# Three token blocks enter the first projection unnormed, and the gate activations run in two parts around their remaking

## The chip, the core and the metric

The kernel runs on one core of a Trainium2 chip. The core has a matrix engine (TensorE, PE), a vector engine (VectorE, DVE), an activation engine (ScalarE, ACT), a general engine (GpSimd, POOL) and one that only issues transfers here (SyncE, SP). Each runs its own instructions and waits on the others by semaphores. The metric is the device time of one execution in microseconds (us).

## What is computed

One layer of a hybrid decoder, for 1024 prompt tokens and 32 decode tokens (8 sequences of 4), model width 1024, all in float32. Cut to what matters here:

```python
h = rmsnorm(x, norm_w)                      # x * rsqrt(mean(x*x) + eps) * norm_w
proj = einsum('btd,dc->btc', h, w_in)       # one projection, 4104 columns
hq, hf, hi, hgate, fq, fk, fv, ff, fgate = split(proj)
hg_o, S = hgrn_chunked(q(hq), k(hf), log_f(hf), v=hi, s0)   # gated linear recurrence
fox_o = fox attention over fq, fk, fv, log_sigmoid(ff + b)  # forgetting softmax attention
hg = rmsnorm(hg_o, hg_norm_w) * silu(hgate)
fx = fox_o * silu(fgate)
y = rmsnorm(x + concat(hg, fx) @ w_out, final_norm_w)
```

The norm of a token is one factor for its whole row, so a projection of `x * norm_w` can be multiplied by that factor afterwards.

## The kernel before

**Tiling.** The prompt is 8 blocks of 128 tokens (`tb` 0 to 7), the decode rows are a ninth. A block of x lies with the model dimension on the partitions, as 8 slices `k` of 128 x 128 (`xts[tb]`). A float32 product is made as three matmuls of rounded parts: `hi` holds the rounded value, `lo` the rest, and `proj` issues `xhi*hi`, `xhi*lo`, `xlo*hi` for each of the 8 slices, 24 matmuls per block and result bank. A weight slice is split into parts by `split` (a copy, L351 or L353, and a subtraction, L354), a token block by `norm_hi`/`norm_lo` (L269, L273).

**Order.** The order of the instructions on each engine is the order of the code (a manual schedule); pools only add waits. In time:

1. The start. `load_x` and `w1.load` transfer x and the first projection's weights (512 columns, `hi` of the reference, values of the recurrence) in four pairs of slices. Block 0 and block 1 enter it unnormed: `quick_hi`/`quick_lo` (L282, L286) make the parts of `x * norm_w`, `quick_sq`/`quick_r` (L290 and eight matmuls against a column of ones) give `rc`, the factor of each token, and the copy out of the bank multiplies by it (L424, L435). Matmuls of 128x128 ones keep PE busy before (`warm`).
2. Blocks 2 to 7 and the decode rows enter normed. `norm_a` squares a block (ACT, L243), multiplies it by norm_w (POOL, L245) and sums the squares per token (DVE, L249); `norm_b` sums over the partitions with one matmul of ones, makes the factor (ACT, L218 and L219), multiplies (DVE, L265) and makes the parts (L269, L273). It stands for the next block after the first nine matmuls of a block.
3. The gate loop, `gate_group(tb)` for blocks 2 to 7, 0, 1: 48 matmuls of 260 columns into two banks, copied out by DVE (L526 the first bank, L529 adds a bias to 8 columns of the second, L530 copies the rest of it). The same two banks serve the next group. Then `again` remakes blocks 0 and 1 with the norm in, in three steps, one behind each of the first six groups: square, norm_w and sums (L304, L306, L307); the sum over the partitions, the factor and the product (L218, L219, L313); the parts (L269, L273). Then `silu_mul` (ACT L379, L380, L381; DVE L382; ACT L383; POOL L384, L386) acts on the gate in place. The first of the 24 slabs of 128 columns is split behind groups 4 and 6 (L486 on ACT, L487 on DVE). After the last group come `log_sigmoid` of the forget gates (L536 to L545) and the gates of the decode rows (`proj_d`, 32 matmuls; L369, L370).
4. The slabs (`slab`, 24 matmuls on each of three stretches of 352 columns), with the recurrence and the attention woven in, then the output. They read the parts of all blocks, normed.

`U(i)` are reused buffers of one kind. `wk` holds `ones` and small sums, and the same buffer is `silu_mul`'s scratch later (in order listings it is `u_103`).

Of the kernel before, what the change touches and what calls it, by code (L numbers as in the profile page):

```python
# [70 lines left out]
def tile_hymba(ctx, tc, x_prompt, x_sample, x_b, x_d, cache_k_t, cache_v, cache_logf_t, state_hgrn, page_table,  # L71
               norm_w, w_1, w_2, w_s, b_fox_f, hg_lb, hg_norm_w, w_out, final_norm_w, consts,
# [54 lines left out]
    def ps_s():  # L127
        return bank("ps", 3)
# [103 lines left out]
    warm(14)  # L232
# [46 lines left out]
    rc = cst.tile([128, 2], F32, name="rc")  # L279
# [52 lines left out]
    class Group:  # L332
# [12 lines left out]
        def split(self, kp, ce=(A, A), se=(V, G)):  # L345
# [3 lines left out]
            for a in range(2):  # L349
# [25 lines left out]
    def silu_mul(x, n):  # L375
# [10 lines left out]
        G.tensor_mul(x3, x3, hw[:n, None, :].to_broadcast([n, NH, HK]))  # L386

# [51 lines left out]
    for tb in range(2, NB):  # L439
        if tb < 6:  # L440
            norm_a(tb + 2)
# [3 lines left out]
        w1.proj(ps, tb, every, range(3))  # L445
# [107 lines left out]
    anew = [again(0), again(1)]  # L553
    for n, tb in enumerate((2, 3, 4, 5, 6, 7, 0, 1)):
        gate_group(tb)
        if n < 6:
            next(anew[n // 3])
# [7 lines left out]
        silu_mul(sg[tb // 2][:, tb % 2], 128)  # L565
# [9 lines left out]
    silu_mul(sgd[:, :512], ND)  # L575
# [981 lines left out]
```

## Time and profile before

| | us |
|---|---|
| runs, three | 773.49, 775.08, 773.97 |
| median | 773.97 |
| profiled execution | 775.96 |
| its span, first to last instruction | 774.20 |
| mean granted clock of PE | 0.985 |

The span is what the profile's times count from; the profiled execution took 1.76 us more. Its rows below are of two kinds. A row of the timeline gives start, length, engine, source line, operation, what is written and read, shape and count, and in brackets how long the engine sat idle before it and who ended that. A row of the waits or of a stretch gives sums.

### The profile page before, as it was taken

The page shows a single profiled execution, that of the slowest core. Times are in us where ns is not written, and L with a number is a line of the kernel's source. Part 1 is how long each engine was busy: PE and PEld are TensorE (multiplying, and loading weights), DVE is VectorE, ACT ScalarE, POOL GpSimd, SP SyncE. Part 2 cuts the span into 40 slices and gives each one's busy share as a digit, 9 for nine tenths or more (in the row PEclk, how much of TensorE's full clock was granted, in tenths as well). Part 3 has the DMA queues.
Part 4 walks back from the last instruction along what each step waited for, and adds up shares of the span by engine and source line. Part 5 has one row for each costly group of instructions (what it writes and reads, how often), then busy time and mean ns, then how long its engine had stood idle before and what let it go on. Part 6 is the DMA issues. An engine that isn't in the chain of part 4 may idle for free.

```text
span 774.2 us, 13013 instructions
## 1 busy us (share of the span) xinstructions
PE 741.8 (96%) x4835; PEld 665.5 (86%) x4835; DVE 464.8 (60%) x973; ACT 363.5 (47%) x853; POOL 315.1 (41%) x332
## 2 busy tenths in 40 slices
PE   8999989999999999998999899989999899999996
PEld 7778989998999999998998899979988776577886
DVE  5775554747647565366447844785478776667422
ACT  5663555434242431136546654757466521555322
POOL 0442544364371753726434552536344533232101
PEclk9999999999999999999999999999999999999999
DMA  8211000101221113013001021101111596713521
GB/s 337 93 36 40 1 11 20 60 4 58 82 83 58 55 33 110 28 37 134 28 29 57 29 71 40 57 30 55 55 57 57 188 329 221 260 58 123 199 81 55
DMA packets 27569, 64.99 MB, mean 84 GB/s; under 512 B 5394, under 2 KB 6546, under 8 KB 27506
## 3 DMA queue, kind: packets, MB, share of 16 engines
q1 hardware_dynamic: 27506, 64.16, 24.3%
q8 instruction: 38, 0.62, 0.3%
q14 instruction: 25, 0.20, 0.1%
HBM read 47.27 MB, written 16.88 MB: 83 GB/s over the span
## 4 chain that ended last, share of the span: by engine, by line
PE 73%; DVE 13%; ACT 8%; issue 3%; DMA 2%; POOL 1%; SPq 1%; DVEq 0%; ACTq 0%; POOLq 0%
PE pj L95 53%; PE ps L95 11%; PE po L95 3%; PE pt L965 2%; DVE u L970 2%; DVE u L896 1%; PE pt L95 1%; DVE st L935 1%; ACT u L969 1%; ACT u L945 1%; DMA u<-in_x_prompt_dram 1%; DMA u<-in_w_dram 1%; ACT xhi L269 1%; DVE u L831 1%; DVE u L638 1%
## 5 line engine op out<-in xcount | busy, mean ns | idle before, releaser
L95 PE MATMUL pj<-xhi,u 128*128 128x352 f32 x1152 | 307.2, 331 | 0.9 <-DVE u L487 0.5
L95 PEld LDWEIGHTS pj<-xhi,u 128*128 128x128 f32 x1152 | 206.5, 190 | 3.1 <-DVE u L487 0.8
L95 PE MATMUL pj<-xlo,u 128*128 128x352 f32 x576 | 187.3, 325 | 0.0
L95 PE MATMUL ps<-u,u 128*128 128x64 f32 (+6 forms) x984 | 129.2, 272 | 3.5 <-ACT u L945 2.6
L95 PEld LDWEIGHTS ps<-u,u 128*128 128x128 f32 (+2 forms) x984 | 112.2, 178 | 12.9 <-ACT u L945 4.4
L950 POOL TENSOR_SCALAR u<-u,st 128x128 f32<-128x128 f32 (+3 forms) x64 | 48.7, 762 | 153.4 <-DVE st L948 87.7
L95 PEld LDWEIGHTS pj<-xlo,u 128*128 128x128 f32 x576 | 109.6, 190 | 0.7
L95 PE MATMUL pj<-u,xhi 128*128 128x260 f32 (+1 forms) x384 | 91.7, 332 | 5.7 <-DVE u L526 3.4
L945 ACT ACTIVATE u<-ps,st 128x512 f32<-128x512 f32 (+2 forms) x96 | 55.0, 578 | 50.3 <-DVE st L938 21.4
L95 PEld LDWEIGHTS pj<-u,xhi 128*128 128x128 f32 x384 | 65.2, 195 | 13.9 <-DVE u L526 3.0
L95 PE MATMUL pj<-h,u 128*128 128x512 f32 (+2 forms) x237 | 74.1, 384 | 0.8 <-DVE h L1086 0.8
L699 POOL TENSOR_TENSOR u<-u,u 128x256 f32<-128x256 f32 (+1 forms) x56 | 42.0, 751 | 76.5 <-PE ps L95 76.4
L970 DVE TENSOR_TENSOR u<-pt,u 128x512 fp32r<-128x512 f32 (+1 forms) x80 | 48.5, 632 | 28.4 <-ACT u L969 27.9
L95 PE MATMUL pj<-u,xlo 128*128 128x260 f32 (+1 forms) x192 | 63.8, 333 | 0.0
L969 ACT ACTIVATE u<-pt 128x512 fp32r<-128x512 f32 (+1 forms) x80 | 41.8, 552 | 41.1 <-PE pt L965 33.5
L935 DVE TENSOR_REDUCE st<-ps 128x1 f32<-128x512 f32 (+2 forms) x96 | 53.4, 556 | 12.2 <-PE ps L95 9.6
L95 PE MATMUL po<-u,u 128*128 128x256 f32 (+1 forms) x320 | 52.2, 287 | 8.5 <-DVE u L970 4.5
L95 PEld LDWEIGHTS po<-u,u 128*128 128x128 f32 x320 | 44.3, 189 | 15.4 <-DVE u L970 7.5
L95 PEld LDWEIGHTS pj<-h,u 128*128 128x128 f32 (+1 forms) x237 | 42.4, 186 | 10.3 <-issue 1.5
L95 PE MATMUL pj<-u,u 128*128 128x512 f32 (+3 forms) x174 | 46.1, 434 | 2.4 <-ACT u L1253 1.0
L95 PE MATMUL pj<-w,u 128*128 128x512 f32 (+2 forms) x125 | 47.4, 380 | 0.0
L700 POOL TENSOR_TENSOR u<-u,u 128x256 f32<-128x256 f32 (+1 forms) x56 | 43.6, 778 | 0.0
(252 smaller groups left out, 1147.0 us busy)
## 6 DMA issues: line engine op xcount, KB each, us to landing
u<-in_w_s_dram SPq DMA_DIRECT2D x24, 512.0 KB
out_dram<-u SPq DMA_DIRECT2D x12, 512.0 KB
u<-in_x_b_dram SPq DMA_DIRECT2D x8, 512.0 KB
u<-in_cache_k_t_dram SPq DMA_DIRECT2D x16, 256.0 KB
u<-in_cache_v_dram SPq DMA_DIRECT2D x16, 256.0 KB
m_s<-u SPq DMA_DIRECT2D x7, 512.0 KB
u<-m_s SPq DMA_DIRECT2D x14, 256.0 KB
w<-in_w_out_dram SPq DMA_DIRECT2D x12, 256.0 KB
```

The source lines that it names most:

```text
L95: PE.matmul(out, lhsT, rhs, start=start, stop=stop, skip_group_check=True)
L269: A.activation(xhi[:, k, t0:t0 + n], xt[:, k], AF.Copy)
L638: V.tensor_mul(f, f3[:, :, 0], f3[:, :, 1])
L699: G.tensor_mul(k4[:, :, 0, :], k4[:, :, 0, :], f3[:, eb, 1:2].to_broadcast([128, n, m]))
L700: G.tensor_mul(q4[:, :, 1, :], q4[:, :, 1, :], f3[:, eb, 0:1].to_broadcast([128, n, m]))
L831: V.tensor_copy(hi, vo[:, :, 64 * i:64 * i + 64])
L935: V.tensor_reduce(st[:, m:m + 1], ps, axis=AX.X, op=OP.min)
L945: A.activation(P[:, s], ps, AF.Exp, scale=-1.0, bias=st[:, lo:lo + 1], accum_out=st[:, 2 + m:3 + m])
L950: G.tensor_scalar(P[:, :e], P[:, :e], st[:, 4:5], 1.0, op0=OP.mult, op1=OP.mult)
L965: PE.transpose(p[:, c:c + 128], probs[n, b][:, j * 128:(j + 1) * 128], ident)
L969: A.activation(ph[:, :w], p[:, :w], AF.Copy)
L970: V.tensor_sub(pl[:, :w], p[:, :w], f32(ph[:, :w]))
```

## The change

Three blocks, 0 to 2, enter unnormed. Blocks 0 and 1 go side by side: for each slice `k` the three matmuls of block 0 are followed by the three of block 1, into two banks, and the weights are split slice by slice, all copies on ACT. Block 1's transfer moves ahead of the second weight pair, and norm_w comes as 8 more columns of block 0's transfer (`x_0`); `nwc` is a copy of it. Neither `quick_sq` nor `quick_r` is left: the results stay unscaled in `v`. The loop over the other blocks starts with block 2, unnormed. `again` now also makes `rc`, by a second matmul into the same bank, and scales `v`; it is there for blocks 0, 1 and 2, one step behind each of groups 1 to 7, with two steps behind groups 3 and 5 (the last of one block and the first of the next). The gate loop takes blocks 3 to 7, 0, 1, 2; block 2's input is transferred a second time. `silu_mul` is a generator: Abs, Exp and Ln are issued before the step of `again`, the rest after it.

```diff
     xts = {}
 
     def load_x(tb):
         n = 128 if tb < NB else ND
-        xts[tb] = U((17, 18, 24, 25, 26, 27, 24, 25, 26)[tb], D, a=KB)[:, :, :n]
-        SP.dma_start(xts[tb], (x_b[tb] if tb < NB else x_d).rearrange("p (k t) -> p k t", k=KB))
+        t = U((17, 18, 24, 25, 26, 27, 25, 26, 27)[tb], D + KB if tb == 0 else D)
+        xts[tb] = t[:, :D].rearrange("p (a b) -> p a b", a=KB)[:, :, :n]
+        if tb == 0:
+            SP.dma_start(t, x_0)
+        else:
+            SP.dma_start(xts[tb], (x_b[tb] if tb < NB else x_d).rearrange("p (k t) -> p k t", k=KB))
+
+
+    nwT = U(17, D + KB)[:, D:]
...
-    rc = cst.tile([128, 2], F32, name="rc")
+    rc = cst.tile([128, 3], F32, name="rc")
...
-    def quick_sq(tb):
-        A.activation(U(15 + tb % 2, D, a=KB), xts[tb], AF.Square)
-
-    def quick_r(tb):
-        sq, p = U(15 + tb % 2, D, a=KB), ps_s()[:, :1]
-        for k in range(KB):
-            mm(p, sq[:, k], ones[:, :1], k == 0, k == KB - 1)
-        rstd(rc[:, tb:tb + 1], p, D)
+    nwc = cst.tile([128, KB], F32, name="nwc")
 
     def again(tb):
 
         xt, sq = xts[tb], U(7, D, a=KB)
-        on, s, r = (U(6)[:, i * 128:i * 128 + 128] for i in range(3))
+        on, s, r = (U(6)[:, i * 128:i * 128 + 128] for i in (0, 2 * tb + 1, 2 * tb + 2))
         if tb == 0:
             V.memset(on, 1.0)
         A.activation(sq, xt, AF.Square)
...
         yield
-        p = ps_s()[:, :128]
-        mm(p, on, s, True, True)
-        rstd(r, p, D)
+        p = ps_s()[:, :129]
+        mm(p[:, :128], on, s, True, True)
+        mm(p[:, 128:], s, on[:, :1], True, True)
+        rstd(r, p[:, :128], D)
+        rstd(rc[:, tb:tb + 1], p[:, 128:], D)
         for k in halves:
             V.tensor_mul(xt[:, k], xt[:, k], r[:, None, :].to_broadcast([128, 4, 128]))
         yield
         for f in (norm_hi, norm_lo):
             for k in halves:
                 f(tb, k)
+        x = v[tb // 2][:, tb % 2]
+        A.activation(x, x, AF.Copy, scale=rc[:, tb:tb + 1])
         yield
...
         A.activation(t, t, AF.Ln, bias=1.0)
+        yield
         V.scalar_tensor_tensor(t, x, 0.0, t, op0=OP.min, op1=OP.subtract)
         A.activation(t, t, AF.Exp)
         G.tensor_mul(x, x, t)
         x3 = x.rearrange("p (h v) -> p h v", h=NH)
         G.tensor_mul(x3, x3, hw[:n, None, :].to_broadcast([n, NH, HK]))
+        yield
...
     load_x(0)
-    SP.dma_start(nwT, norm_w)
     w1.load(0)
+    load_x(1)
     w1.load(1)
-    load_x(1)
     w1.load(2)
     w1.load(3)
-    load_x(2)
-    load_x(3)
-    ks = range(KB)
-    for k in ks:
-        quick_hi(0, k)
-    for k in ks[:4]:
-        quick_lo(0, k)
-    w1.split(0, (V, V), (V, V))
-    quick_sq(0)
-    for k in ks[4:]:
-        quick_lo(0, k)
-    w1.split(1, (A, A), (V, V))
-    load_x(4)
-    load_x(5)
+    for tb in range(2, 6):
+        load_x(tb)
     SP.dma_start(cc, consts[:, :K_MK])
     pa, pb = ps_pj(), ps_pj()
-    w1.proj(pa, 0, every, ks[:4])
-    w1.split(2, (A, A), (V, V))
-    w1.proj(pa, 0, every, ks[4:6])
-    w1.split(3, (A, A), (V, V))
-    quick_r(0)
-    for k in ks:
-        quick_hi(1, k)
-    w1.proj(pa, 0, every, ks[6:])
-    for k in ks:
-        quick_lo(1, k)
-    A.activation(v[0][:, 0], pa, AF.Copy, scale=rc[:, 0:1])
+
+    def quick(tb, *ks):
+        for k in ks:
+            quick_hi(tb, k)
+            quick_lo(tb, k)
+
+    for k in range(0, KB, 4):
+        quick(0, *range(k, k + 4))
+        for i in range(k, k + 4):
+            w1.split(i // 2, (A, A), (V, V), (i % 2,))
+            if i < k + 2:
+                quick(1, i)
+            if i == k + 1:
+                quick(1, k + 2, k + 3)
+            w1.proj(pa, 0, every, (i,))
+            w1.proj(pb, 1, every, (i,))
+    V.tensor_copy(nwc, nwT)
+    quick(2, *range(KB))
+    norm_a(3)
+    A.activation(v[0][:, 0], pa, AF.Copy)
     w2.load(0)
     w2.load(1)
-    red = norm_sq(2)
-    quick_sq(1)
-    red(0)
-    w1.proj(pb, 1, every, ks)
-    norm_b(2)
-    quick_r(1)
-    norm_a(3)
-    load_x(6)
-    A.activation(v[0][:, 1], pb, AF.Copy, scale=rc[:, 1:2])
+    A.activation(v[0][:, 1], pb, AF.Copy)
     w2.load(2)
     SP.dma_start(bf, bcast_row(b_fox_f, FH))
     SP.dma_start(hw, bcast_row(hg_norm_w, HK))
     for tb in range(2, NB):
-        if tb < 6:
+        if 2 < tb < 6:
             norm_a(tb + 2)
         if tb == 7:
             w1.proj_d(vd, every)
         ps = ps_pj()
-        w1.proj(ps, tb, every, range(3))
+        w1.proj(ps, tb, every, range(4 if tb == 2 else 3))
         if tb == 6:
             norm_b(NB)
         if tb < 7:
             norm_b(tb + 1)
-        if tb < 4:
-            load_x(tb + 5)
+        if tb == 2:
+            norm_a(4)
+        if tb < 5:
+            load_x(tb + 4)
         if tb == 5:
             norm_a(NB)
-        w1.proj(ps, tb, every, range(3, 6))
+        w1.proj(ps, tb, every, range(4 if tb == 2 else 3, 6))
         if tb < 5:
             w2.split(tb - 2)
         if tb == 3:
...
-    anew = [again(0), again(1)]
-    for n, tb in enumerate((2, 3, 4, 5, 6, 7, 0, 1)):
+    anew = [again(tb) for tb in range(3)]
+
+    xts[2] = U(2, D, a=KB)
+    SP.dma_start(xts[2], x_b[2].rearrange("p (k t) -> p k t", k=KB))
+    for n, tb in enumerate((3, 4, 5, 6, 7, 0, 1, 2)):
         gate_group(tb)
-        if n < 6:
-            next(anew[n // 3])
+        si = silu_mul(sg[tb // 2][:, tb % 2], 128)
+        next(si)
+        for i in range(3):
+            if 2 * i <= n <= 2 * i + 2:
+                next(anew[i])
         if n == NB - 1:
             log_sigmoid(lf.rearrange("p b h -> p (b h)"), zf.rearrange("p b h -> p (b h)"), 128, 64)
             V.tensor_copy(lfh, lf.rearrange("p b h -> p h b"))
@@ -562,7 +562,7 @@
             w2.proj_d(sgd[:, 260:], slice(260, 520))
         if n in (3, 4, 5):
             next(lbs)
-        silu_mul(sg[tb // 2][:, tb % 2], 128)
+        next(si)
```

Two places on ACT, one on PE and one on DVE show what moved.

ACT at the start of the program, before (`u_121` and `u_128` are blocks 0 and 1, `u_126`, `u_130`, `u_132` weight pairs 2 to 4, whose first pair DVE splits):
```order
L282 ACTIVATE xhi<-u_121,nwT 128x128 x8
L290 ACTIVATE u_154<-u_121 128x1024
L351 ACTIVATE u_160<-u_126 128x512 x2
L351 ACTIVATE u_183<-u_130 128x512 x2
L351 ACTIVATE u_195<-u_132 128x512 x2
L218 ACTIVATE rc<-ps_202,eps 128x1
```

and after (`u_72` is block 0 with norm_w, `u_124` block 1, `u_122`, `u_126`, `u_128` pairs 1 to 3):
```order
L287 ACTIVATE xhi<-u_72 128x128 x4
L353 ACTIVATE u_147<-u_122 128x512
L287 ACTIVATE xhi<-u_124,u_72 128x128
L353 ACTIVATE u_147<-u_122 128x512
L287 ACTIVATE xhi<-u_124,u_72 128x128 x3
L353 ACTIVATE u_173<-u_126 128x512 x2
L287 ACTIVATE xhi<-u_72 128x128 x4
L353 ACTIVATE u_199<-u_128 128x512
```

Block 1's parts stand between the copies of the weights, and the square and the factor are gone.

PE, the end of block 0 in the start, before (`pj` are result banks, `u_103` holds the column of ones, `u_154` the squares):
```order
L95 MATMUL pj_170<-u_183,xlo 128x512
L95 MATMUL ps_202<-u_103,u_154 128x1 x8
L95 MATMUL pj_170<-u_195,xhi 128x512
L95 MATMUL pj_170<-u_196,xhi 128x512
L95 MATMUL pj_170<-u_195,xlo 128x512
```

and its first six matmuls after `warm` in the changed kernel:
```order
L95 MATMUL pj_138<-u_147,xhi 128x512
L95 MATMUL pj_138<-u_148,xhi 128x512
L95 MATMUL pj_138<-u_147,xlo 128x512
L95 MATMUL pj_137<-u_147,xhi 128x512
L95 MATMUL pj_137<-u_148,xhi 128x512
L95 MATMUL pj_137<-u_147,xlo 128x512
```

The eight one-column matmuls are gone, and two banks take turns slice by slice.

DVE, the fourth group of the gate loop up to the emptying of the fifth's first bank, before (`u_627` and `u_628` squares and sums, `u_831` the slab's high part):
```order
L526 COPY u_101<-pj_169 128x260
L529 TENSOR_TENSOR zf<-pj_170,bf 128x8
L530 COPY u_101<-pj_170 128x252
L307 TENSOR_REDUCE u_628<-u_627 128x128
L511 TENSOR_TENSOR lb<-lb 128x4
L382 SCALAR_TENSOR_TENSOR u_103<-u_101,u_103 128x512
L487 TENSOR_TENSOR u_832<-u_124,u_831 128x512
L526 COPY u_102<-pj_169 128x260
```

and after:
```order
L520 COPY u_102<-pj_137 128x260
L523 TENSOR_TENSOR zf<-pj_138,bf 128x8
L524 COPY u_102<-pj_138 128x252
L313 TENSOR_TENSOR u_124<-u_124,u_613 128x512 x2
L505 TENSOR_TENSOR lb<-lb 128x4
L385 SCALAR_TENSOR_TENSOR u_103<-u_102,u_103 128x512
L481 TENSOR_TENSOR u_826<-u_122,u_825 128x512
L520 COPY u_102<-pj_137 128x260
```

The products of block 1's second step stand there instead of its first step's sums.

ACT, the seventh group of the gate loop and the start of the eighth's activations, before (`u_99` is their gate buffer):
```order
L379 ACTIVATE u_103<-u_99 128x512
L380 ACTIVATE u_103<-u_103 128x512
L381 ACTIVATE u_103<-u_103 128x512
L383 ACTIVATE u_103<-u_103 128x512
L536 ACTIVATE u_128<-zf 128x64
```

and after (`u_556` is block 2, `u_96` its projection):
```order
L381 ACTIVATE u_103<-u_99 128x512
L382 ACTIVATE u_103<-u_103 128x512
L383 ACTIVATE u_103<-u_103 128x512
L274 ACTIVATE xhi<-u_556 128x4x128 x2
L319 ACTIVATE u_96<-u_96,rc 128x512
L386 ACTIVATE u_103<-u_103 128x512
L381 ACTIVATE u_103<-u_100 128x512
```

The high parts of block 2 are written here, behind the seventh group's Ln; the eighth group is block 2's. In the eighth group Abs, Exp and Ln now stand ahead of the log-sigmoid.

## Rows read from the trace of the kernel before

**Rows 1.** The page: busy us of each engine, its share, instructions.
```profile
PE 741.8 (96%) x4835; PEld 665.5 (86%) x4835; DVE 464.8 (60%) x973; ACT 363.5 (47%) x853; POOL 315.1 (41%) x332
```

**Rows 2.** Gate loop and decode rows: busy PE, PEld, DVE, ACT, POOL; clock; DMA.
```profile
68.70:124.40 55.70, 52.29 (x421) 51.91 (x420) 30.73 (x62) 25.80 (x47) 24.63 (x19) 0.97 0.03 11
```

**Rows 3.** PE's waits up to 130 us: total, times, longest.
```profile
PE pj L95 <- DVE u L526: 3.4, 2, 2.8
```

**Rows 4.** Three stretches, columns as in rows 2; the clock is third from the end.
```profile
10.20:13.60 3.40, 3.27 (x8) 2.07 (x8) 3.38 (x9) 1.91 (x4) 0.00 (x0) 0.50 1.02 416
27.20:30.60 3.40, 3.40 (x9) 2.26 (x8) 2.76 (x3) 2.70 (x5) 2.11 (x3) 0.50 0.51 143
102.30:105.70 3.40, 3.40 (x19) 3.40 (x18) 2.03 (x7) 2.56 (x6) 0.94 (x1) 0.50 0.00 0
```

**Rows 5.** Timeline of the start: start us, us, engine, line, operation.
```profile
4.76 2.45 ACT L282 ACTIVATE xhi<-u,nwT 128x128 fp32r<-128x128 f32 x8 [2.74 <-DMA nwT<-in_norm_w_dram]
...
7.72 0.43 DVE L353 CAST u<-u 128x512 fp32r<-128x512 f32 x1 [1.30 <-DMA u<-in_w_dram]
...
9.00 1.15 ACT L351 ACTIVATE u<-u 128x512 fp32r<-128x512 f32 x2 [0.85 <-DMA u<-in_w_dram]
...
10.90 3.89 DVE L354 TENSOR_TENSOR u<-u,u 128x512 fp32r<-128x512 f32 x6
...
17.88 2.40 DVE L286 SCALAR_TENSOR_TENSOR xlo<-u,nwT,xhi 128x128 fp32r<-128x128 f32 x8 [3.08 <-ACT xhi L282]
...
18.36 0.62 PE L95 MATMUL pj<-u,xhi 128*128 128x512 f32 x2
...
19.05 0.63 PE L95 MATMUL pj<-u,xhi 128*128 128x512 f32 x2
...
24.12 1.84 PE L95 MATMUL ps<-u,u 128*128 128x1 f32 x16
...
40.21 0.30 PEld L95 LDWEIGHTS pj<-u,xhi 128*128 128x128 f32 x2 [0.35 <-ACT xhi L269]
```

**Rows 6.** Timeline of the gate loop and the decode rows, several engines.
```profile
74.69 0.17 DVE L529 TENSOR_TENSOR zf<-pj,bf 128x8 f32<-128x8 f32 x1 [2.00 <-issue]
...
75.28 0.64 ACT L379 ACTIVATE u<-u 128x512 f32<-128x512 f32 x1 [4.85 <-DVE u L530]
...
77.27 0.69 DVE L382 SCALAR_TENSOR_TENSOR u<-u,u 128x512 f32<-128x512 f32 x1
...
80.61 0.37 ACT L218 ACTIVATE u<-ps,eps 128x128 f32<-128x128 f32 x1 [1.98 <-PE ps L95]
...
81.42 1.30 DVE L313 TENSOR_TENSOR u<-u,u 128x512 f32<-128x512 f32 x2 [0.54 <-POOL u L386]
...
84.47 1.14 ACT L269 ACTIVATE xhi<-u 128x512 fp32r<-128x512 f32 x2
...
90.21 1.04 ACT L304 ACTIVATE u<-u 128x1024 f32<-128x1024 f32 x1
...
92.53 2.03 DVE L307 TENSOR_REDUCE u<-u 128x128 f32<-128x1024 f32 x1
...
99.11 1.34 DVE L487 TENSOR_TENSOR u<-u,u 128x512 fp32r<-128x512 f32 x1 [1.21 <-ACT u L486]
...
99.98 1.61 POOL L386 TENSOR_TENSOR u<-u,hw 128x512 f32<-128x512 f32 x1
...
100.84 0.51 PE L95 MATMUL pj<-u,xhi 128*128 128x260 f32 x2 [2.79 <-DVE u L526]
...
120.61 4.00 PE L95 MATMUL pj<-u,xd 128*64 128x260 f32 x32
...
120.81 0.17 DVE L529 TENSOR_TENSOR zf<-pj,bf 128x8 f32<-128x8 f32 x1 [2.46 <-PE pj L95]
...
121.59 0.20 DVE L538 TENSOR_SCALAR u<-u 128x64 f32<-128x64 f32 x1 [0.29 <-ACT u L537]
...
123.89 0.41 DVE L370 TENSOR_TENSOR sgd<-sgd,pj 32x260 f32<-32x260 f32 x1
```

More of the change, by code (lines that the diff above doesn't have):

```diff
@@ L70, in tile_hymba @@
 @with_exitstack
-def tile_hymba(ctx, tc, x_prompt, x_sample, x_b, x_d, cache_k_t, cache_v, cache_logf_t, state_hgrn, page_table,
-               norm_w, w_1, w_2, w_s, b_fox_f, hg_lb, hg_norm_w, w_out, final_norm_w, consts,
+def tile_hymba(ctx, tc, x_prompt, x_sample, x_0, x_b, x_d, cache_k_t, cache_v, cache_logf_t, state_hgrn, page_table,
+               w_1, w_2, w_s, b_fox_f, hg_lb, hg_norm_w, w_out, final_norm_w, consts,
                y_prompt, y_sample, k_t, prompt_v, prompt_logf, prompt_state,
@@ L180, in need @@
         debt[0] = max(debt[0], -3.0)
-    A.preload_act_table_set("natural_log_exp_and_others")
-    nwT = cst.tile([128, KB], F32, name="nwT")
     xts = {}
@@ L188, in load_x @@
         n = 128 if tb < NB else ND
-        xts[tb] = U((17, 18, 24, 25, 26, 27, 24, 25, 26)[tb], D, a=KB)[:, :, :n]
-        SP.dma_start(xts[tb], (x_b[tb] if tb < NB else x_d).rearrange("p (k t) -> p k t", k=KB))
+        t = U((17, 18, 24, 25, 26, 27, 25, 26, 27)[tb], D + KB if tb == 0 else D)
[5 more added lines that the diff above has]
+    nwT = U(17, D + KB)[:, D:]
+    A.preload_act_table_set("natural_log_exp_and_others")
     cc = cst.tile([128, K_MK], F32, name="cc")
@@ L230, in warm @@
             mm(pw[:, :128], ones, ones, True, True)
-    warm(14)
+    warm(13)
     ss_ = {}
@@ L244, in norm_sq @@
         for k in (slice(0, 4), slice(4, 8)):
-            G.tensor_mul(xt[:, k], xt[:, k], nwT[:, k, None].to_broadcast([128, 4, n]))
+            G.tensor_mul(xt[:, k], xt[:, k], nwc[:, k, None].to_broadcast([128, 4, n]))
         def reduce(a):
@@ L305, in again @@
         for k in halves:
-            G.tensor_mul(xt[:, k], xt[:, k], nwT[:, k, None].to_broadcast([128, 4, 128]))
+            G.tensor_mul(xt[:, k], xt[:, k], nwc[:, k, None].to_broadcast([128, 4, 128]))
         V.tensor_reduce(s, sq.rearrange("p k t -> p t k"), axis=AX.X, op=OP.add)
         yield
-        p = ps_s()[:, :128]
-        mm(p, on, s, True, True)
-        rstd(r, p, D)
+        p = ps_s()[:, :129]
[3 more added lines that the diff above has]
+        rstd(rc[:, tb:tb + 1], p[:, 128:], D)
         for k in halves:
@@ L343, in load, with split @@
             SP.dma_start(raw, self.w[kp].rearrange("p (a c) -> p a c", a=2))
-        def split(self, kp, ce=(A, A), se=(V, G)):
+        def split(self, kp, ce=(A, A), se=(V, G), parts=(0, 1)):
             raw = self.raw[kp]
@@ L348, in split @@
             l = U(self.hl[2 * kp + 1], 2 * self.n, F32R, a=2)
-            for a in range(2):
+            for a in parts:
                 if ce[a] is A:
@@ L574, in tile_hymba @@
         G.tensor_copy(m8[:, l], mk[:, l:l + 1].to_broadcast([128, 4, 64]))
-    silu_mul(sgd[:, :512], ND)
+    for _ in silu_mul(sgd[:, :512], ND):
+        pass
     def log_forget():
@@ L1523, in pairs @@
         return a.reshape(4, 2, 128, -1).transpose(0, 2, 1, 3).reshape(4, 128, -1)
+    x_b = np.asarray(x_prompt)[0].reshape(NB, 128, KB, 128).transpose(0, 3, 2, 1).reshape(NB, 128, D)
     ins = dict(
         x_prompt=x_prompt, x_sample=x_sample,
-        x_b=np.asarray(x_prompt)[0].reshape(NB, 128, KB, 128).transpose(0, 3, 2, 1).reshape(NB, 128, D),
+        x_0=np.concatenate([x_b[0], np.asarray(norm_w).reshape(KB, 128).T], 1), x_b=x_b,
         x_d=np.asarray(x_sample).reshape(ND, KB, 128).transpose(2, 1, 0).reshape(128, KB * ND),
@@ L1532 @@
         state_hgrn=np.asarray(state_hgrn)[0].transpose(1, 2, 0, 3).reshape(NH, 128, DB * 128),
-        page_table=page_table, norm_w=np.asarray(norm_w).reshape(KB, 128).T,
+        page_table=page_table,
         w_1=pairs(w[:, C_HI:C_HI + 512]),
```

## The prediction, made before the changed kernel ran

> **What bounds the kernel now.** I read the page first: TensorE (PE) is busy 741.8 us, 96% of the span [rows 1], so a microsecond is won or lost only where PE idles or runs at half its clock. The change touches the first 125 us. In the gate loop and the decode rows behind it PE is busy 52.29 of 55.70 us [rows 2]. The list of PE's waits up to 130 us names that loop's own: 3.4 us in two waits, 2.8 the longest, for VectorE (DVE) line 526, the copy that empties a gate bank [rows 3]. [...] The timelines of the start [rows 5] and of the gate loop [rows 6] give the durations.
>
> **The start.** Removed: two sums of squares, 16 records of one-column matmuls each, 1.84 us a time [rows 5], 3.7 us on PE's path. Moved: block 1's input lands in the slot where the second weight pair landed. The chain to the first matmuls is then: first pair there at 7.7; ScalarE (ACT) copies slice 0 (two took 1.15, say 0.6 each) to 8.3; block 1 there at 9.0, its first high part to 9.4; slice 1's copy to 9.95; its low part on DVE, 0.65 (six took 3.89), to 10.65. By then PE has done 7 of the 48 matmuls of blocks 0 and 1; before it DVE has 11 low parts of x at 0.30 and 6 of weights at 0.65, done at 17.9, and ACT 11 at 0.31 and 6 at 0.6, done at 17.0 [rows 5]. PE takes longer: three matmuls start in 0.69 (18.36 to 19.05), 0.23 each, and twice that at half clock. I keep the half-clock stretch 10.2 to 13.6, since PE idles before it as now [rows 4]: 6 matmuls to 13.6, the other 35 in 8.05, end 21.65. PE, not the splitting, sets this end; it needs the last slice at 20.3. Copying out block 0 ends 0.2 later and holds block 2, which is unnormed too and has its parts ready by then. Block 2 takes 24 x 0.23 and 0.15 for a sum, to 27.5. Block 3's norm starts behind 12 of its matmuls and needs about 2.6: there at 27.2, no wait. Then a wait: block 4's square follows block 3's high parts on ACT (27.8 + 1.04 [rows 6]), its reduce takes 2.03 on DVE, so its sum is there at 30.9, and PE reaches it behind nine matmuls of block 3 at 29.6: 1.3 idle. Fifteen matmuls more and the 0.35 wait that block 4 has now: it starts at 34.85, against 40.21 [rows 5], **5.4 us earlier**. Cross-check: 3.7 of one-column matmuls and 1.7 of the half-clock stretch 27.2 to 30.6 behind the second of them make 5.4. Blocks 4 to 7 keep order and pace. Bounds: 3.6 if the clock falls behind the new 1.3 wait (1.7 less), 8.4 if that wait and the first half-clock stretch both go (1.3 and 1.7 more). norm_w now rides in block 0's rows, and ACT's first copy waited 2.74 for its landing [rows 5], but what PE needs next is the weight pair at 7.7: nothing. The copy of norm_w, one warming matmul fewer and the reload of block 2 (on the queue of SyncE ahead of the first slab, which is split only in the fourth group) lie beside longer work: nothing.
>
> **The gate loop.** The change reorders the queues of DVE and ACT, and each of these engines waits at the head of its queue. Call E the moment DVE adds the bias (line 529) of a group, which first reads the second bank. PE's own pace is 48 matmuls, 5.7 us a group; E goes from 74.69 to 120.81 over seven groups, 46.1 us with the waits and one half-clock stretch [rows 6]. Now ACT's Abs, Exp and Ln stand ahead of every step of the remaking. They begin 0.6 behind E (74.69 to 75.28), and Ln ends at E + 2.6 (DVE's product starts at 77.27). Before, the remaking had that time. Behind E + 2.6 the steps add up so [rows 6]:
> - sum step (groups 2, 4, 6): Ln and Exp for r 0.7, two multiplications 1.30, the gate's product 0.6: E + 5.3, then the next bank is emptied. In group 2 this is inside PE's own time (6.1 with the sums). In groups 4 and 6 the first slab's split stands behind: final Exp 0.63, copy 0.6, subtraction 1.34, emptying 0.37; the next E is at +8.4 and +8.3.
> - write-and-square step (groups 3 and 5): high parts 1.14, the new scaling of v 0.55 (half of that pair, the nearest row), square 1.04, reduce 2.03, product 0.6, emptying 0.37: +8.2, and +8.9 with four small lower-bound operations.
> - group 1: square, reduce and product behind Ln: +6.6.
> - group 7: the block remade in it (block 2) is the very one that group 8 reads. PE is done at E - 0.3, needs the first half of the high part, E + 3.2, then waits 0.5 more for the low part; 5.74 of matmuls and 0.27 to DVE: +9.7.
>
> Sum: 6.6 + 6.1 + 8.2 + 8.4 + 8.9 + 8.3 + 9.7 = 56.2 against 46.1, **10.1 us more**. The same sums for the order of before give 44.3, with its half-clock stretch 46.0, so I give them 1.5 either way. In groups 3 to 6 DVE's queue is the bound: the emptying copy is queued behind multiplications and a reduce that wait for ACT, and PE waits for the copy. **The tail**: the log-sigmoid's ACT part comes behind Ln (DVE takes it up at E + 3.2) instead of at E + 0.8 (121.59 - 120.81), so the bank that slab 0 needs is emptied at E + 5.9 instead of E + 3.5 (123.89 + 0.41 - 120.81), while PE's 32 decode matmuls end near 124.4, E + 3.6: **2.3 us more**. In slab 0 ACT has less left to do: 0 to 0.5 back, I take 0.3. **The clock**: now PE's 2.79 idle [rows 6] is followed by a half-clock stretch [rows 4], already in the 46.1. The changed loop has waits of 2 to 3 in groups 3 to 6, where a slow PE hides behind DVE, 5.6 before group 8 and 2.3 before slab 0; behind these two PE is the bound. Between 0 and 3.4; I take 3.2, nearest to what followed the 2.79.
>
> Sum: -5.4 + 10.1 + 2.3 - 0.3 + 3.2 = **+9.9 us**. The profiled execution took 775.96, 1.76 around its span of 774.20; the median of the runs shown, 773.97, is 2.0 below it, and I add the difference to the median: 783.9. The ends of all terms together are +2 (start 8.4, loop 8.6, no clock loss) and +14 (start 3.6, loop 11.6).
>
> **Rivals.** (a) Faster: DVE empties the banks in time. If the multiplications' wait for ACT does not hold groups 3 to 6, their waits go, those of now too (2.8 and 0.6, and 1.7 of clock), and group 8's wait of 4.0 and the tail stay: -5.4 - 5.1 + 4.0 + 2.3 + 0.5 of clock = -3.7, 770.3. It decides at whether the next bank is emptied by E + 5.7. For it: ACT is busy only 25.80 of 55.70 [rows 2], and a slip in the order of events would count in four groups. Against it: the subtraction of 99.11 alone made DVE so late that PE stood 2.79 us until 100.84 [rows 6], and it stays. 0.07. (b) Half hidden: groups 3 to 6 cost 4.5 to 9.5 us less, because the sums stack waits that overlap: 774.4 to 779.4. 0.15. (c) The start doesn't do what it says: PE waits slice by slice for ACT and DVE, and the clock stays low for a second stretch; 3.5 of the gain go: 787.4. For it: ACT's weight copies queue behind its wait for block 1. Against it: 17.9 against 20.3 above. 0.10. (d) GpSimd beside DVE: a 128x512 subtraction took 1.34 (99.11) with a GpSimd product next to it (99.98), where six took 0.65 each [rows 5, 6]. If six more of DVE's two-input operations in the loop fall so, 0.65 each, the chain grows by 3.9: 787.8. Against it: GpSimd's two products follow the final Exp, when DVE mostly copies or reduces. 0.08. The forecast has the other 0.60.
>
> [...]
>
> **How the numbers follow.** A measurement of this kernel can tell about 0.2%, 1.5 us, from no change. Faster by more: (a), 0.07. Within it, 772.4 to 775.5: the low end of (b), 0.04. Slower: 0.89. The range reaches from inside (b) to just beyond (c) and (d), 776.5 to 788.5; it leaves out (a), the low part of (b) and the far ends of (c) and (d).
>
> **What would show it.** Block 4's first matmul near 35 us and no one-column records before it, or the start's step is wrong. E of the first and of the eighth group 56 us apart; PE's waits in the loop led by the high part of the remade block, 5 to 6 us at once, and by the emptying copy; slab 0's first matmul 2 to 3 us late for the decode rows' addition. If the eight E lie 46 to 50 apart, the queue argument is wrong, and so is the sign.

## The result, and the profile of the changed kernel

The changed kernel takes 781.64 us (median of 4 runs, 779.46 to 782.50) against 773.73 for the kernel before: a ratio of 1.0096, 95% interval 1.0071 to 1.0121, 7.9 us slower. The forecast was 9.9 us slower. The profiled execution of the changed kernel is the lowest of its four (779.46, its span 777.7), while that of before (775.96) lay 2.2 above the median of 773.73; the two profiles therefore differ by only 3.5 us, and the terms below are compared place by place.

First the page and the stretches, columns as in [rows 1], [rows 2] and [rows 4]: the gate loop with the decode rows, the stretch that ran at half clock before, and the two that do so now.

```profile
PE 738.9 (95%) x4807; PEld 662.2 (85%) x4807; DVE 465.5 (60%) x980; ACT 366.9 (47%) x866; POOL 314.6 (40%) x332
```

```profile
61.19:130.40 69.21, 59.08 (x429) 57.39 (x427) 32.98 (x68) 33.41 (x65) 26.05 (x21) 0.90 0.05 19
10.20:13.60 3.40, 3.40 (x17) 2.64 (x16) 3.40 (x10) 3.40 (x11) 0.00 (x0) 1.00 1.04 418
...
115.60:119.00 3.40, 3.34 (x14) 3.11 (x15) 1.90 (x3) 1.77 (x4) 0.72 (x1) 0.50 0.02 5
119.00:122.40 3.40, 3.40 (x19) 3.40 (x19) 0.43 (x1) 0.00 (x0) 1.84 (x2) 0.57 0.00 0
```

PE has lost 2.9 us of busy time and the kernel is slower. In the loop it idles 10.1 of 69.2 us, against 3.4 of 55.7 in [rows 2]. The stretch from 10.2 to 13.6 holds 17 matmuls at full clock where [rows 4] had 8 at half. PE's waits up to 135 us, as in [rows 3], name new causes beside the emptying copy (line 520 now): the high parts of a remade block, 3.3 us at once, the reduce of the remaking, and the decode rows' addition.

```profile
PE pj L95 <- ACT xhi L274: 3.6, 2, 3.3
PE pj L95 <- DVE u L520: 2.6, 4, 1.1
PE ps L95 <- DVE u L305: 2.4, 2, 1.4
PE pj L95 <- DVE sgd L372: 2.0, 1, 2.0
```

The timeline of the start, to be read beside [rows 5]:

```profile
5.76 0.63 ACT L353 ACTIVATE u<-u 128x512 fp32r<-128x512 f32 x1
...
6.45 0.50 PE L95 MATMUL pj<-u,xhi 128*128 128x512 f32 x1
...
27.92 0.49 PE L95 MATMUL ps<-u 128*128 128x128 f32 x2 [0.97 <-DVE u L254]
...
31.95 0.73 PE L95 MATMUL pj<-u,xhi 128*128 128x512 f32 x2
...
33.34 0.50 PE L95 MATMUL pj<-u,xlo 128*128 128x512 f32 x1 [0.66 <-DVE xlo L278]
```

The copy of the first weight slice begins at 5.76, so that pair had landed by then; before, its copy waited until 7.72. Block 4 starts at 31.95 against 40.21. Now DVE's timeline of the gate loop, its additions of the bias only (the moment E of each group):

```profile
67.22 0.17 DVE L523 TENSOR_TENSOR zf<-pj,bf 128x8 f32<-128x8 f32 x1 [2.52 <-PE pj L95]
...
73.64 0.15 DVE L523 TENSOR_TENSOR zf<-pj,bf 128x8 f32<-128x8 f32 x1
...
79.85 0.17 DVE L523 TENSOR_TENSOR zf<-pj,bf 128x8 f32<-128x8 f32 x1 [0.80 <-PE pj L95]
...
87.92 0.15 DVE L523 TENSOR_TENSOR zf<-pj,bf 128x8 f32<-128x8 f32 x1
...
95.96 0.15 DVE L523 TENSOR_TENSOR zf<-pj,bf 128x8 f32<-128x8 f32 x1
...
104.61 0.16 DVE L523 TENSOR_TENSOR zf<-pj,bf 128x8 f32<-128x8 f32 x1
...
112.57 0.15 DVE L523 TENSOR_TENSOR zf<-pj,bf 128x8 f32<-128x8 f32 x1
...
124.70 0.17 DVE L523 TENSOR_TENSOR zf<-pj,bf 128x8 f32<-128x8 f32 x1 [2.71 <-PE pj L95]
```

From the third to the seventh the steps are 8.07, 8.04, 8.65 and 7.96 where PE alone needs some 6, and only three of the eight additions stand behind a wait for PE: DVE reaches the others without one, straight from the work before them in its queue. The last step is 12.13. The chain of waits shows its links (start, us, what):

```profile
115.09 0.53 ACT xhi L274
...
115.66 9.01 PE pj L95 x48
...
127.25 0.15 ACT u L530
...
130.09 0.33 DVE sgd L372
130.41 0.04 issue
130.46 0.59 PE pj L95 x2
```

The kernel before at two of these places, the first matmul of its eighth group and of slab 0:

```profile
114.78 0.48 PE L95 MATMUL pj<-u,xhi 128*128 128x260 f32 x2 [0.63 <-DVE u L526]
...
124.44 0.34 PE L95 MATMUL pj<-xhi,u 128*128 128x352 f32 x1
```

ACT begins block 2's high parts at 115.0, behind the seventh group's Ln; PE starts the eighth group at 115.66, and its addition follows 9.0 us later (124.70), where it took 6.0 before (114.78 to 120.81): the low clock costs 3.0. Slab 0 starts at 130.46, 5.76 behind the last addition, against 3.63 before (124.44 - 120.81).

Where the time went, from the two profiles: the start gives 7.47 at the first addition (74.69 to 67.22), the loop takes 11.36 more (57.48 against 46.12), the tail 2.13 more; slab 0 starts 6.02 later. Behind it the code is the same, and these two executions differ by 2.5 the other way (649.8 and 647.2 us): 0.9 are two waits of PE near slab 0 that are gone, the rest is not the change's doing as far as the runs show.

### The profile page after: what moved, and what is told of

Same layout as the page of the kernel before. It is cut to its first block, busy times and chain, and to the rows that moved or that the text cites. A ratio compares the mean times of both kernels' runs of the same rounds, so it can differ in the third digit from the quotient of the medians.

```text
span 777.7 us, 12973 instructions
## 1 busy us (share of the span) xinstructions
PE 738.9 (95%) x4807; PEld 662.2 (85%) x4807; DVE 465.5 (60%) x980; ACT 366.9 (47%) x866; POOL 314.6 (40%) x332
## 4 chain that ended last, share of the span: by engine, by line
PE 65%; DVE 14%; ACT 5%; issue 2%; POOL 1%; DVEq 0%; ACTq 0%; POOLq 0%
PE pj L95 46%; PE ps L95 11%; PE po L95 3%; PE pt L966 2%; DVE u L897 2%; DVE u L971 2%; DVE st L936 2%; PE pt L95 1%; ACT u L946 1%; ACT u L970 1%; DVE u L853 1%; DVE u L832 1%; DVE u L998 1%; DVE u L639 1%; DVE ps L935 0%
## 5 line engine op out<-in xcount | busy, mean ns | idle before, releaser
L95 PE MATMUL pj<-xhi,u 128*128 128x352 f32 x1152 | 304.1, 328 | 2.0 <-DVE sgd L372 2.0
L95 PEld LDWEIGHTS pj<-xhi,u 128*128 128x128 f32 x1152 | 204.3, 188 | 3.9 <-DVE sgd L372 2.2
L95 PE MATMUL ps<-u,u 128*128 128x64 f32 (+7 forms) x952 | 125.7, 273 | 3.5 <-ACT u L946 2.6
L95 PEld LDWEIGHTS ps<-u,u 128*128 128x128 f32 (+2 forms) x952 | 108.4, 178 | 12.9 <-ACT u L946 4.4
L95 PE MATMUL pj<-u,xhi 128*128 128x260 f32 (+1 forms) x384 | 93.7, 337 | 6.6 <-ACT xhi L274 3.6
L95 PEld LDWEIGHTS pj<-u,xhi 128*128 128x128 f32 x384 | 67.4, 202 | 14.7 <-ACT xhi L274 5.3
L95 PEld LDWEIGHTS po<-u,u 128*128 128x128 f32 x320 | 44.3, 188 | 16.2 <-DVE u L971 7.6
```

Of the source, the lines that this page charges most:

```text
L95: PE.matmul(out, lhsT, rhs, start=start, stop=stop, skip_group_check=True)
```

## The experiments

**e1: the gate activation whole again, behind the remaking step.** Start, third block and spread stay.

```diff
         si = silu_mul(sg[tb // 2][:, tb % 2], 128)
-        next(si)
         for i in range(3):
...
             next(lbs)
+        next(si)
         next(si)
```

> The gate activation is whole again and stands behind the remaking step, as before the change; the new start, the third remade block and the spread over seven groups stay. Theory (order of ACT's queue): the loop lost its 11.4 us because Abs, Exp and Ln stand ahead of each remaking step. Then the eight additions of the bias lie 46.6 us apart by the same sums, 48.3 with one half-clock stretch, instead of 57.5; the log-sigmoid is ahead of the gate activation again, so slab 0 starts 3.6 us behind the last of them instead of 5.8; together 11 us less than the changed kernel, about 770.5 us, and below the kernel before. Rival (the third block and the spread cost it): the additions stay over 54 us apart and the time stays over 777.

Measured: 771.65 us, 0.9957 (0.9938 to 0.9975) of the kernel before. Its timeline: the first and last addition, the one long wait of PE, one pair of DVE's multiplications with the GpSimd products beside it, and slab 0's subtraction.

```profile
66.86 0.17 DVE L523 TENSOR_TENSOR zf<-pj,bf 128x8 f32<-128x8 f32 x1 [2.02 <-issue]
...
117.43 0.17 DVE L523 TENSOR_TENSOR zf<-pj,bf 128x8 f32<-128x8 f32 x1 [2.46 <-PE pj L95]
```

```profile
94.72 0.77 PE L95 MATMUL pj<-u,xhi 128*128 128x260 f32 x2 [3.76 <-DVE u L520]
```

```profile
85.87 2.92 DVE L313 TENSOR_TENSOR u<-u,u 128x512 f32<-128x512 f32 x2 [0.62 <-ACT u L224]
...
92.89 1.34 DVE L481 TENSOR_TENSOR u<-u,u 128x512 fp32r<-128x512 f32 x1 [1.22 <-ACT u L480]
```

```profile
85.25 1.28 POOL L387 TENSOR_TENSOR u<-u,u 128x512 f32<-128x512 f32 x1 [2.35 <-ACT u L386]
86.61 1.63 POOL L389 TENSOR_TENSOR u<-u,hw 128x512 f32<-128x512 f32 x1
```

The additions lie 50.57 us apart instead of 57.48, and slab 0 starts 3.62 behind the last (121.05). So the order of ACT's queue it is: one changed place takes 10 us off, and this version beats the kernel before. The loop is 2.3 longer than expected. The sums knew nothing of the 2.92: DVE's two multiplications take 1.29 in the changed kernel, and so do two of the three pairs here; the pair shown takes 2.92, from 85.87 to 88.79, where GpSimd's products of the group before run beside it (85.25 to 88.24). ACT's next Abs stands behind a lower-bound operation that waits for this pair on DVE, so the 1.6 pass on to the emptying copy. Then come one longer wait of PE (3.76, from 90.96 to 94.72) and a half-clock stretch twice as long as expected (93.2 to 100.0). How the 2.3 divide between the two is not shown.

**e2: norm_w by a transfer of its own again**, second in SyncE's queue.

```diff
     load_x(0)
+    SP.dma_start(nwT, norm_w)
     w1.load(0)
```

> norm_w comes by a transfer of its own again, second in SyncE's queue, as before the change; all else as in the changed kernel. Theory: this 4 KB transfer of short packets held up what is queued behind it, so the first weight pair lands at 7.7 instead of before 5.8; then PE's first real matmul is at 8.3 instead of 6.45, the half-clock stretch behind it returns, the first bias addition comes 2 to 3 us later than 67.2, and the kernel takes 2 to 3 us more, 784. Rival (the order of the transfers of x and w alone makes the gain): no more than 0.5 us, and PE's first matmul stays before 6.8.

Measured: 785.09 us, 1.0117 (1.0082 to 1.0152) of before. Timeline and stretches of its start:

```profile
7.91 0.63 ACT L349 ACTIVATE u<-u 128x512 fp32r<-128x512 f32 x1 [2.27 <-DMA u<-in_w_dram]
...
8.60 1.52 PE L95 MATMUL pj<-u,xhi 128*128 128x512 f32 x2 [2.79 <-ACT u L349]
```

```profile
6.80:10.20 3.40, 1.60 (x3) 1.07 (x4) 1.07 (x3) 1.61 (x4) 0.00 (x0) 0.64 1.00 387
10.20:13.60 3.40, 3.40 (x9) 2.63 (x9) 3.40 (x10) 3.40 (x10) 0.00 (x0) 0.50 1.03 420
```

The first weights are 2.1 us later, PE idles 2.79 and then runs at half clock for two stretches; the first addition stands at 71.39 instead of 67.22. Without this part the new start gains 3.3 us, not 7.5. The difference in time, 1.6 by the ratios and 3.4 by the medians, lies about the expected 2 to 3, but the two intervals overlap; the timeline is what decides.

**e7: the same part alone, in the kernel before.**

```diff
-    SP.dma_start(nwT, norm_w)
...
         if tb == 0:
             SP.dma_start(t, x_0)
```

> The kernel before with one part of the change alone: norm_w rides in block 0's rows. Theory: without its own 4 KB transfer the weights land nearly 2 us earlier, PE's first real matmul comes at about 6.5 instead of 8.3, and the half-clock stretch from 10.2 to 13.6 goes; the later ends of the start are set by PE, so 1.5 to 3 us come off, a ratio of 0.996 to 0.998. Rival (only the new order of the start can use earlier weights): within 0.5 us of the kernel before.

Measured: 0.9978 (0.9959 to 0.9996), some 1.7 us. PE's first real matmul is at 6.54 and its first addition at 72.34 instead of 74.69; no stretch at half clock before 24.6. As expected, and by the timeline not the rival; by the time alone it is less clear, since the interval ends at 0.9996, 0.3 us, within the rival's 0.5. The loop, whose code is that of before, took 44.56 us here instead of 46.12: PE waited 2.75 us for the emptying copy, as before, but no half-clock stretch followed. So the prediction's sum for the order of before without such a stretch, 44.3, is borne out.

```profile
6.54 0.47 PE L95 MATMUL pj<-u,xhi 128*128 128x512 f32 x1 [0.35 <-ACT xhi L287]
```

**e3: the log-sigmoid ahead of the gate activation in the last group**, else the changed kernel.

```diff
         gate_group(tb)
+        if n == NB - 1:
+            log_sigmoid(...)
         si = silu_mul(sg[tb // 2][:, tb % 2], 128)
```

> In the last group the log-sigmoid is issued ahead of the gate activation's first part; all else as in the changed kernel. Theory: the 2.1 us by which slab 0 starts later behind the last bias addition (5.8 against 3.6) come from Abs, Exp and Ln ahead of the log-sigmoid on ACT; they go, and the kernel takes about 2 us less, 779.5. Rival: the copies of the decode rows on ACT or the chain on DVE set it, and slab 0 stays 5 to 6 us behind.

Measured: 779.13 us, 1.0040 (1.0016 to 1.0065). The last addition and slab 0:

```profile
123.66 0.17 DVE L523 TENSOR_TENSOR zf<-pj,bf 128x8 f32<-128x8 f32 x1 [2.46 <-PE pj L95]
...
127.68 0.43 PE L95 MATMUL pj<-xhi,u 128*128 128x352 f32 x1 [0.23 <-DVE sgd L372]
```

Slab 0 starts 4.02 behind the addition instead of 5.76, and PE's wait for the decode rows' addition falls from 2.0 to 0.23. The order named is the cause. The ratio moved by 4.3 us, more than the 1.74 that the edit can be seen to give; part of the rest (0.75) is that the eighth group came sooner, the remainder stays open.

**e4: the last remaking step left out**, so that the eighth group waits for nothing fresh; block 2 stays unnormed behind the first projection.

```diff
-            if 2 * i <= n <= 2 * i + 2:
+            if 2 * i <= n <= min(2 * i + 2, 5):
```

> The last remaking step, which writes block 2's parts in the seventh group, is left out, so block 2 stays unnormed in everything behind the first projection; this time is no candidate, it prices the wait of the eighth group. Theory: that group's 12.1 us fall to 6.1 (7.8 if the clock still falls once behind the emptying copy), the two half-clock stretches from 115.6 to 121.4 go or become one, and the kernel takes 4.3 to 6 us less, 775.6 to 777.3. Rival (the eighth group waits for the emptying copy in any case): 2 us less at most.

Measured: 776.93 us, 1.0030 (1.0011 to 1.0050), 5.1 less than the changed kernel by the ratios. The seventh and eighth addition, and the stretch of the eighth group:

```profile
112.35 0.15 DVE L523 TENSOR_TENSOR zf<-pj,bf 128x8 f32<-128x8 f32 x1
...
118.57 0.17 DVE L523 TENSOR_TENSOR zf<-pj,bf 128x8 f32<-128x8 f32 x1 [2.46 <-PE pj L95]
```

```profile
112.20:118.60 6.40, 6.12 (x50) 6.12 (x51) 1.77 (x6) 2.53 (x4) 3.21 (x3) 1.00 0.28 84
```

6.22 us instead of 12.13, at full clock: reading block 2 right behind its remaking cost 2.9 of waiting (PE waits 0.34 here, 3.27 in the changed kernel) and 3.0 of clock. The edit also takes the step's work out of the queues of ACT and DVE, but that is not what PE stood for: in the changed kernel the first bank was empty from 112.65, and PE waited on for the high part until 115.66.

**e8: the two parts alone, in the kernel before**, with two blocks remade in six groups.

```diff
         gate_group(tb)
+        si = silu_mul(sg[tb // 2][:, tb % 2], 128)
+        next(si)
         if n < 6:
...
-        silu_mul(sg[tb // 2][:, tb % 2], 128)
+        next(si)
```

> The kernel before with one part of the change alone: the gate activation in two parts around the remaking step, with two blocks remade in six groups as before. Theory (order of ACT's queue): the sums give 48.4 us between the additions against 44.3, with two half-clock stretches instead of one +1.7, and slab 0 starts 2.1 us later; 6 to 8 us more, a ratio of 1.008 to 1.010. Rival (the two parts hurt only with the third block and its tighter spread): less than 3 us more.

Measured: 779.65 us, 1.0062 (1.0039 to 1.0085). Its timeline:

```profile
73.93 0.17 DVE L531 TENSOR_TENSOR zf<-pj,bf 128x8 f32<-128x8 f32 x1 [2.52 <-PE pj L95]
...
123.14 0.17 DVE L531 TENSOR_TENSOR zf<-pj,bf 128x8 f32<-128x8 f32 x1 [2.46 <-PE pj L95]
```

```profile
101.49 0.50 PE L95 MATMUL pj<-u,xhi 128*128 128x260 f32 x2 [3.08 <-DVE u L528]
```

49.21 us between the additions against 46.12, and 2.13 more in the tail (slab 0 at 128.90): 5.2, and 4.8 by the ratio (3.0 to 6.6). A little under the expected 6 to 8, in part since only one half-clock stretch fell in the loop where two were expected, and over the rival's 3 by the profile; the interval begins there. A second stretch stands behind PE's wait before slab 0 (129.0 to 135.8, clock 0.69 and 0.80). The order hurts by itself; with the third block, the denser steps and the eighth group's wait the 3.1 in the loop are 11.4.

**e5: as e1, slab 0's subtraction on GpSimd.**

```diff
-            (V if i < 11 else G).tensor_sub(...)
+            (V if 0 < i < 11 else G).tensor_sub(...)
```

> As the run with the whole gate activation behind the remaking step (e1), but the subtraction of slab 0's split in the fourth and sixth group goes to GpSimd instead of VectorE. Theory: with the activation whole, what is left of the loop's waits comes from that 1.36 us subtraction standing on VectorE ahead of the emptying copy (3.8 us at one place, with 6.8 us at half clock behind it). The additions of the bias then lie 43.8 us apart by the sums, 45.5 with one half-clock stretch, instead of 50.6, and the kernel takes 4 to 6 us less than e1: a ratio of 0.988 to 0.990 to the kernel before. Rival (GpSimd and VectorE hold each other up): GpSimd's subtraction lands beside VectorE's two-input operations, these take up to 1.3 instead of 0.65, and less than 2 us come off.

Measured: 769.66 us, 0.9942 (0.9917 to 0.9966). The loop, columns as in [rows 2], and a pair of DVE's multiplications:

```profile
67.16:114.00 46.84, 43.09 (x350) 42.12 (x349) 32.74 (x49) 28.12 (x55) 27.21 (x20) 1.00 0.04 12
```

```profile
86.17 2.90 DVE L313 TENSOR_TENSOR u<-u,u 128x512 f32<-128x512 f32 x2 [0.63 <-ACT u L224]
```

The loop is 3.7 shorter and without a half-clock stretch, but the time moved by only 1.2 by the ratios. Since the two intervals overlap, both kernels were run once more, side by side.

> The kernel of e1 once more, beside e10 on one chip, since the medians of e1 and e5 were taken apart and their intervals overlap. Theory (its own profile: additions 50.6 us apart, 6.8 us at half clock): a ratio of 0.995 to 0.997 to the kernel before.

> The kernel of e5 once more, beside e9. Theory (the profiles of e1 and e5 differ by 3.4 us at the start of slab 0): 3 to 4 us less than e9, a ratio of 0.990 to 0.992. Rival (GpSimd's subtraction gives back what it takes off VectorE, since VectorE's pairs of operations took 2.4 to 2.9 us instead of 1.3 beside GpSimd): less than 1.5 us under e9.

Measured: e9 771.25 us, 0.9963 (0.9951 to 0.9974); e10 769.20 us, 0.9932 (0.9909 to 0.9955). 2.4 us by the ratios, between theory and rival; the intervals still overlap a little. In this execution of e10 the additions lie 49.0 apart (66.97 to 115.98), a half-clock stretch from 101.7 to 105.1 among them; in the profile of e5 there was none. So the subtraction was a cause of the longer loop; in this execution a part of what it frees is lost again.

**e6: as e5, and the remaking begun before the loop.** Block 0 is remade and block 1's sum taken during the last two blocks of the first projection; block 2 follows in groups two to four.

```diff
+        if tb == 6:
+            next(anew[0])
+            next(anew[1])
...
-        for i in range(3):
-            if 2 * i <= n <= 2 * i + 2:
-                next(anew[i])
+        for i in ((1,), (1, 2), (2,), (2,), (), (), (), ())[n]:
+            next(anew[i])
```

> As e5, and the remaking begins before the gate loop: block 0 is remade, and block 1's sum taken, while the last two blocks of the first projection run on TensorE, block 1 is finished in the first two groups and block 2 in the second to fourth; block 2's input is still where it landed and is not loaded again. Theory: VectorE and ScalarE idle from 52.9 to 60.3, so the steps there cost nothing, no group reads a block that has just been remade, and no wait is left in the loop: additions 40.9 us apart, no half-clock stretch, slab 0 near 111.5 instead of 121.05 in e1; 9 us less than e1, a ratio of 0.983 to 0.986 to the kernel before. Rival (the split of the last weight pair, which PE needs at 63, comes late behind the remaking): a wait of 1 to 3 us before 66 and a half-clock stretch give back 2 to 4 us.

Measured: 763.64 us, 0.9868 (0.9831 to 0.9904): 10.2 us below the kernel before and 18 below the changed one. Windows of the work before the loop and of the loop:

```profile
52.00:67.60 15.60, 15.60 (x95) 13.08 (x94) 12.12 (x14) 7.93 (x15) 5.34 (x5) 1.00 0.19 48
```

```profile
67.69:109.83 42.14, 41.68 (x346) 41.38 (x345) 24.07 (x43) 24.80 (x47) 23.69 (x18) 1.00 0.04 14
```

PE is busy throughout the first, although DVE now works 12.1 of its 15.6 us, and idles 0.46 us in the loop, where the changed kernel had 8.2 in its 57.48. Slab 0 starts at 113.45, 17 us earlier than in the changed kernel. The ratio ends just above the expected 0.983 to 0.986, and the additions lie 42.1 apart and not 40.9; the rival's late weight pair did not come.

**e11: as e6, the subtraction on VectorE.**

```diff
-            (V if 0 < i < 11 else G).tensor_sub(...)
+            (V if i < 11 else G).tensor_sub(...)
```

> As e6, but slab 0's subtraction is back on VectorE. It tells how much of e6 is the early remaking and how much the subtraction's engine. Theory: with no step of the remaking left in the groups with the split, the subtraction costs VectorE 1.3 us twice, of which the sums leave waits of 2.4 and 0.9 us and a half-clock stretch: additions 44 to 46 us apart instead of 42.1, a ratio of 0.989 to 0.992. Rival (the early remaking alone does it): within 1 us of e6, 0.987 to 0.988.

Measured: 768.85 us, 0.9934 (0.9918 to 0.9950). PE's wait in the loop:

```profile
94.60 0.51 PE L95 MATMUL pj<-u,xhi 128*128 128x260 f32 x2 [2.89 <-DVE u L530]
```

The additions lie 45.51 apart, as expected, though the kernel is some 1 us slower than the expected ratio. Over e1 (0.9957 and 0.9963) the early remaking alone gives some 0.3%, as the subtraction on GpSimd alone does (e10), and both together 0.9%. The two 0.3 are hardly more than the intervals tell apart, the 0.9 is well beyond them. Each alone leaves waits of PE: 2.89 for the emptying copy here, 1.83 for it and 1.86 for a remade block's low parts in e10.

## Why the prediction was right, step by step

- **The start: right in sign and mechanism, 5.4 forecast, 8.3 measured at the same place** (block 4, 40.21 to 31.95), and 7.5 left of it at the first addition. The failed step is the sentence that set norm_w's ride in block 0's rows at nothing because "what PE needs next is the weight pair at 7.7". That pair itself was held up by norm_w's transfer: it was there by 5.8. So PE began at 6.45 instead of 8.3, and the half-clock stretch that I kept went too. e2 prices this at 4.2 us on the first addition. My other start, with the pair at 7.7, gains 3.3 in e2 where I had 5.4: PE's wait of 2.79 before its first matmul was followed by two half-clock stretches, not one, which is 1.7 of the difference. The wait for block 4's sum was 0.97 (forecast 1.3), and no stretch fell behind it. "Blocks 4 to 7 keep order and pace" left out 0.66: block 4 waits that long for its low parts (the row at 33.34), which is most of the 0.8 lost up to the first addition. The bounds, 3.6 and 8.4, hold both numbers.
- **The loop: 10.1 forecast beside the new clock loss, 8.4 measured** (11.4 with the 3.0 of clock). Step by step, forecast and measured: 6.6 and 6.42; 6.1 and 6.21; 8.2 and 8.07; 8.4 and 8.04; 8.9 and 8.65; 8.3 and 7.96; 9.7 and 12.13. The last contains the low clock; without it, it is 9.1: PE's wait was 3.27 where the sum has 4.0, since the second wait for the low part did not come. The 5.6 that the prediction names for this wait in its clock term, and the "5 to 6 us at once" among its signs, do not agree with its own sum and were not seen (4.8 in e3). e1, e4 and e8 confirm the causes: ACT's order by itself, the block read behind its remaking, and more cost where the third block makes the steps denser.
- **The tail: 2.3 forecast, 2.13 measured**; e3 moves 1.74 of it.
- **The clock: 3.2 forecast, 3.0 measured, and that they are so close is luck.** The forecast looks to two waits, before the eighth group and before slab 0; in the profile both stretches fell behind the first and none behind the second. In e2, with the same code at both places, one stretch fell behind each. The 1.7 that the forecast counts for a stretch is half of its 3.4 us at a clock of 0.50 [rows 4]; from 10.2 to 13.6, PE ran 8 matmuls at 0.50 in the kernel before and 17 at 1.00 in the changed one. Two more, near 88 and 105, cost PE nothing that shows, as the steps of those groups came out no longer than their sums: DVE was the bound.
- **Slab 0's relief: 0.3 forecast, 0.9 measured.** Two waits of PE in and just behind slab 0, one for ACT and one for a slab's split, stand in the kernel before (below) and are gone in the changed one; e1, with the activation whole, has two of 0.3 and 0.5 again:

```profile
132.75 0.43 PE L95 MATMUL pj<-xhi,u 128*128 128x352 f32 x1 [0.35 <-ACT u L614]
...
137.70 0.59 PE L95 MATMUL pj<-xhi,u 128*128 128x352 f32 x2 [0.52 <-DVE u L487]
```

- **The sum:** 9.9 forecast, 7.9 measured by the medians. Up to slab 0 the forecast is 10.2, and the profiles give 6.0: the start was 2.1 better at the first addition, the loop with its clock 1.9 better than 10.1 + 3.2. The other 1.9 between 6.0 and the medians no run here assigns to a place: the two profiled executions lie 2.2 below and 2.2 above their medians, and where a half-clock stretch falls changes from one execution to the next (one kernel, in the loop: none in e5, one at 101.7 in e10). That 7.9 lies nearer to the forecast than 6.0 does is not the forecast's merit.
- **The rivals.** (a) and (b) did not come: DVE's copy was late in the third to the seventh group, at the cost that the sums gave. (c) did not come; the start did more than it says. (d), GpSimd beside DVE, did not come in the changed kernel, whose pairs take 1.29, and came in some groups where the activation stands last: 2.92 in one pair of three in e1, 2.90 and 2.94 in two of three in e5, 1.62 at most in the kernel before. In e1's trace the long pair ends at 88.79, 0.55 us behind the end of GpSimd's second product (88.24); why the pair takes longer beside GpSimd's products is not shown. So the two parts do shield the remaking from GpSimd here, 1.29 against 2.92 in one pair; e1 shows that the shield costs more than it saves.

## What to carry to other kernels

In these runs what stood ahead in ACT's queue delayed what stood behind it (with the log-sigmoid issued first, in e3, slab 0 starts 4.02 us behind the last addition instead of 5.76). So before splitting an activation around other steps, add up what then stands ahead of the copy that frees the next bank: three activations of 0.63 us, put ahead of a chain that ends in that copy, cost 7 us in eight groups, with the clock (57.48 against 50.57 in e1). Put work that nothing waits for where its engines idle (in e6 some 13 us earlier, under another projection), and let no group read what the group before it has just written (PE waited 3.27 us for it, 0.34 in e4). Look at what a small transfer delays behind it, not only at who waits for its own data (e2: 4.2 us on the first addition).

## What the runs showed of the hardware that was not expected

- The 4 KB transfer of norm_w cost the transfers behind it about 2 us (the first weights' copy begins at 7.72 in the kernel before, 7.91 in e2 and 5.76 in the changed one): the window 4.6 to 6.3 us moved 193 GB/s in the kernel before and 383 in the changed one (last column). With this part alone taken into the kernel before it was 359 (e7), with it taken out of the changed one 277 (e2). Why it holds them up is not shown.

```profile
4.60:6.30 1.70, 1.70 (x10) 1.70 (x9) 1.10 (x4) 1.54 (x6) 0.00 (x0) 1.00 0.74 193
```

```profile
4.60:6.30 1.70, 1.70 (x12) 1.70 (x10) 1.23 (x4) 1.70 (x5) 0.00 (x0) 1.00 1.01 383
```

- Waits of PE of like length were not followed by like clocks: 2.79 us by one stretch of 3.4 at a clock of 0.50 (before), 2.75 at the same place of the same loop by none (e7), 3.76 by two (e1), 3.27 by two (changed), 2.89 by none (e11); the 1.98 before slab 0 by none (changed), 1.97 by one (e2, e8).
- From slab 0 to the end the same instructions took 646.3 us (e4) to 650.3 us (e8), with one and five stretches of 3.4 us at half clock in them. One of e8's five stands behind PE's wait before slab 0. This moves the time by some 0.5%, and is why the ratios of several runs, not two profiles, give the result.
